# A product-key expert layer's scatter: one-hot rows for four tokens in one instruction, and one buffer for the transposed query

## The chip, the core and the metric

One core of a Trainium2 chip. The metric is the device time of one execution in microseconds (us), as the median of several runs. The core's engines are TensorE (PE in the rows, its weight loads PEld), VectorE (DVE), ScalarE (ACT), GpSimd (POOL) and SyncE (SP), which here only issues transfers. Each engine works through its own queue in order and waits on semaphores of the others.

## The reference

One decoder layer on 1024 prompt tokens and 32 sample tokens, model width 1024, in float32. A mixer (dilated softmax attention, gated linear attention, retention) with its output projection comes first; then a product-key expert layer (PEER) and a final norm. What bears on the change is the expert layer:

```python
qk = (xb @ w_pq).reshape(128, 8, 2, 128)           # 8 heads, two half queries
sc = einsum('thpc,pkc->thpk', qk, keys)            # 128 keys per half
s1, i1 = top_k(sc[:, :, 0], 16); s2, i2 = top_k(sc[:, :, 1], 16)
cand = s1[..., :, None] + s2[..., None, :]
top_s, pos = top_k(cand, 16)                       # 16 of 256 per head
eidx = i1 * 128 + i2                               # at pos: one of 16384 experts
gate = softmax(top_s)
pre = einsum('td,ted->te', xb, u_tab[eidx])
out = einsum('te,ted->td', gelu(pre) * gate, v_tab[eidx])
```

So each token uses 8 x 16 = 128 experts, each an index pair (i1, i2) with a gate.

## The kernel before, in words

The tokens lie in nine tiles: 0 to 7 with 128 prompt tokens each, 8 with the 32 sample tokens. They are handled in five groups, [0], [1, 2], [3, 4], [5, 8] and [6, 7]. For each group the input projection (`inproj`), the mixer (`attention`) and then `outproj` are written down, the next group's `inproj` ahead of the present group's `attention`. `outproj` ends with the expert layer's query:

- For each of 8 heads (`m2`), PE multiplies the two half-query weight tiles with the tokens (L661; L301 for the group of one tile) into a PSUM bank of `pj`, of which there are two. `pj` also serves the input and output projections (L343, L383, L631) and the transposes L259. ScalarE copies the result to the tile `qkT` (L662, or L655).
- For each tile of the group, PE multiplies `qkT` with the keys (L667) into `scr`, one bank; ScalarE copies this to `sc` (L670, two buffers); DVE searches the top 16 of each half (`top16`, L684 to L688).
- `select` then makes the 16 pairs and gates of each head, on DVE for the most part.

From here two paths compute the experts. For tiles 0, 1, 6, 7 and 8 (`gather`) GpSimd fetches each chosen row of the two tables by an indirect DMA (L951, L966), and DVE does a multiply-add over 1024 columns with it (L953, L968). For tiles 2 to 5 (`DENSE`, 512 tokens) all 16384 experts are computed as dense matmuls (`dense`), and what is needed is a matrix of gates, experts by tokens. `scatter` makes it. For each token it builds two one-hot matrices over its 128 pairs: `o2`, where column j of row p is 1 if i2 of pair p is j (DVE, L992, two tokens in one instruction), and `o1`, the same for i1 with the gate as its value (ScalarE, two instructions a token, L997 and L998). A matmul of the two (L999) gives the token's 128x128 gates. Four tokens fill the one PSUM bank `sct`; ScalarE copies it to `st` (L1000), and every eight tokens SyncE stores `st` to `gsd` in DRAM (L1001).

`dense` opens when the mixer's memory is given back. It splits weights and activations into a high and a low part (ScalarE L1017, GpSimd or DVE L1018), and runs over 128 groups of 128 experts: three passes of matmuls up (L1044), Gelu (L1045), the product with the gates `Gt` loaded from `gsd` (L1030, L1048), and, four groups at a time, three passes of matmuls down (L1060), added to `oT` on DVE (L1064).

The order within each engine's queue is not that of the text: at build time a list scheduler plans all instructions with estimated durations (line 1160), highest priority first. Attention, scatter (L677) and dense have raised priorities; the gathers (L1107) have the lowest and are put where the plan sees their engines free. The order is fixed from then on. Where a tile's buffers are all in use, the instruction that writes the next one waits for the last reader of the oldest.

Of the kernel before, what the change touches and what calls it, by code (L numbers as in the profile page):

```python
# [9 lines left out]
F32 = mybir.dt.float32  # L10
# [7 lines left out]
OP = mybir.AluOpType  # L18
# [116 lines left out]
def build(tc, I, O):  # L135
    nc = tc.nc
    ctx = ExitStack()
    V, S, G, PE, SP = nc.vector, nc.scalar, nc.gpsimd, nc.tensor, nc.sync
# [6 lines left out]
    wp = mctx.enter_context(tc.tile_pool(name="wp", bufs=1))  # L145
# [9 lines left out]
    def cload(name, shape, src=None, pool=mc):  # L155
        x = pool.tile(shape, F32, name="c_" + name)
        loads.append(lambda: SP.dma_start(x, I[name] if src is None else src))
        return x

    def bcast(ap, n):  # L160
        return bass.AP(tensor=ap.tensor, offset=ap.offset, ap=[[0, 128], [1, n]])
# [11 lines left out]
    iota128 = cload("iota128", [128, 128], pool=con)  # L173
# [18 lines left out]
    def pj():  # L192
        return ps.tile([128, 512], F32, name="pj", bufs=2)
# [7 lines left out]
    def scr_():  # L201
        return ps.tile([128, 512], F32, name="scr", bufs=1) if SCB == 1 else pj()
# [8 lines left out]
    def na(n=1024):  # L211
        return t4(n, "na", 4)
# [23 lines left out]
    def small(shape, dt=F32, name="sm", bufs=4):  # L236
        return sm.tile(shape, dt, name=name, bufs=bufs)
# [7 lines left out]
    def rms(x, n, nm, junk):  # L245
        ss = con.tile([128, 1], F32, name="ss" + nm, bufs=4)
        S.activation(junk[:n], x, AF.Square, scale=1.0 / 32.0, accum_out=ss[:n])  # L247
        return rstd_of(ss, n, nm)

    def rows(t):  # L250
        return (NP, NS) if t == 8 else (t * 128, 128)

    def transpose_to(dst, c0, src, n):
        for half in range(2):
            p = pj()
            for k in range(4):
                kt = half * 4 + k
                sx = src[half][:n, k * 128:(k + 1) * 128] if isinstance(src, tuple) else src[:n, kt * 128:(kt + 1) * 128]
                PE.transpose(p[:, k * 128:k * 128 + n], sx, ident[:n, :n])  # L259
            S.activation(dst[:, half * 4:half * 4 + 4, c0:c0 + n],  # L260
                         p.rearrange("p (k t) -> p k t", t=128)[:, :, :n], AF.Copy)
# [6 lines left out]
    doff, c = {}, 0  # L268
# [4 lines left out]
    def wtile(src):  # L273
        w = wp.tile([128, 1024], F32, name="w", bufs=WB)
        SP.dma_start(w, src)
        return w.rearrange("p (k m) -> p k m", k=8)

    def wn(src):
        r = []
        for q in range(2):  # L280
            w = wp.tile([128, 1024], F32, name="w", bufs=WB)
            SP.dma_start(w, src[:, q * 1024:(q + 1) * 1024])
            w = w.rearrange("p (k m) -> p k m", k=4)
            r += [w[:, k] for k in range(4)]
        return r
# [328 lines left out]
    def outproj(g):  # L614
        tiles, T, off, oa, sil, nt = g.tiles, g.T, g.off, g.oa, g.sil, g.nt
        oT = wp.tile([128, 8, T], F32, name="hT", bufs=2)
        for i, t in enumerate(tiles):
            transpose_to(oT, off[t], (oa[:, i], sil[:, i]), rows(t)[1])
        x1 = [na() for t in tiles]
        for i, t in enumerate(tiles):  # L620
            r0, n = rows(t)
            SP.dma_start(x1[i][:n], I["x"][r0:r0 + n])
        gffn = na()
        SP.dma_start(gffn, bcast(I["g_ffn"], D))
        for c in range(4):
            w = wn(I["w_outc"][c])
            for i, t in enumerate(tiles):
                n = rows(t)[1]
                p = pj()
                for kt in range(8):  # L630
                    PE.matmul(p[:n, :256], oT[:, kt, off[t]:off[t] + n], w[kt], start=kt == 0, stop=kt == 7)  # L631
                d = x1[i][:n, c * 256:(c + 1) * 256]
                V.tensor_tensor(d, d, p[:n, :256], op=OP.add)
        h2T = wp.tile([128, 8, T], F32, name="hT", bufs=2)
        for i, t in enumerate(tiles):
            r0, n = rows(t)
            SP.dma_start(x1d[r0:r0 + n], x1[i][:n])
            h2 = na()
            rs = rms(x1[i][:n], n, "b", h2)
            V.scalar_tensor_tensor(h2[:n], x1[i][:n], rs[:n], gffn[:n], op0=OP.mult, op1=OP.mult)  # L640
            if t not in DENSE:
                SP.dma_start(h2d[r0:r0 + n], h2[:n])
            transpose_to(h2T, off[t], h2, n)
            if t in DENSE:
                c = doff[t]
                SP.dma_start(h2Td[:, :, c:c + n], h2T[:, :, off[t]:off[t] + n])

        tk = {}
        for i, t in enumerate(tiles):
            tk[t] = (t4p["tk"].tile([128, 2, 8, 16], F32, name="tks", bufs=2), t4p["tk"].tile([128, 2, 8, 16], U16, name="tki", bufs=2))  # L650
        for m2 in range(8):
            qkT = wp.tile([128, 2, T], F32, name="qkT", bufs=2)
            if T == 128:
                p = pair_rows("w_pqT", m2 * 2, h2T)
                S.activation(qkT.rearrange("p m t -> p (m t)"), p[:, :256], AF.Copy)  # L655
            else:
                for m in range(2):
                    w = wtile(I["w_pqT"][m2 * 2 + m])
                    p = pj()
                    for kt in range(8):  # L660
                        PE.matmul(p[:, :T], w[:, kt, :], h2T[:, kt], start=kt == 0, stop=kt == 7)  # L661
                    S.activation(qkT[:, m], p[:, :T], AF.Copy)  # L662
            for i, t in enumerate(tiles):
                n = rows(t)[1]
                p = scr_()
                for m in range(2):
                    PE.matmul(p[:n, m * 128:(m + 1) * 128], qkT[:, m, off[t]:off[t] + n],  # L667
                              keysT[:, m * 128:(m + 1) * 128], start=True, stop=True)
                sc = small([128, 256], name="sc", bufs=2)
                S.activation(sc[:n], p[:n, :256], AF.Copy)  # L670
                ts, ti = tk[t]
                for m in range(2):
                    top16(sc[:n, m * 128:(m + 1) * 128], ts[:n, m, m2], ti[:n, m, m2], n, 128)
        for i, t in enumerate(tiles):
            eg = select(t, *tk[t])
            if t in DENSE:
                with tc.high_priority(-SCP):  # L677
                    scatter(t, *eg)
            else:
                peer_q.append((t,) + eg)  # L680
# [294 lines left out]
    def scatter(t, gfl, gate):  # L975
        n = rows(t)[1]
        p = sct_()
        for q in range(2):
            PE.transpose(p[:, q * 128:q * 128 + n], gfl[:n, q], ident[:n, :n])
        PE.transpose(p[:, 256:256 + n], gate[:n].rearrange("p h k -> p (h k)"), ident[:n, :n])  # L980
        tr = small([128, 4, 128], name="tr", bufs=1)
        S.activation(tr[:, :3, :n], p[:, :384].rearrange("p (q t) -> p q t", t=128)[:, :, :n], AF.Copy)
        S.activation(tr[:, 3, :n], p[:, 256:256 + n], AF.Copy, scale=-1.0)
        for b in range(0, n, TB):
            st = t4p["st"].tile([128, 128, TB], F32, name="st", bufs=STB)
            for q in range(0, TB, 4):
                p = sct_()
                c = b + q
                for k in range(4):
                    if k % 2 == 0:  # L990
                        o2 = small([128, 2, 128], name="o2", bufs=2)
                        V.tensor_tensor(o2, iota128[:, None, :].to_broadcast([128, 2, 128]),  # L992
                                                     tr[:, 1, c + k:c + k + 2, None].to_broadcast([128, 2, 128]),
                                                     op=OP.is_equal)
                    i1, gt, ng = (tr[:, x, c + k:c + k + 1] for x in (0, 2, 3))
                    o1 = small([128, 128], name="o1", bufs=O1B)
                    S.activation(o1, iota128, AF.Abs, scale=-1.0, bias=i1)  # L997
                    S.activation(o1, o1, AF.Relu, scale=ng, bias=gt)  # L998
                    PE.matmul(p[:, k * 128:(k + 1) * 128], o2[:, k % 2], o1, start=True, stop=True)  # L999
                S.activation(st[:, :, q:q + 4], p.rearrange("p (k i) -> p i k", k=4), AF.Copy)  # L1000
            SP.dma_start(gsd[(doff[t] + b) // TB], st.rearrange("p i t -> p (i t)"))  # L1001

# [173 lines left out]
```

## Time and profile before

| | us |
|---|---|
| median of 3 runs | 3195.73 |
| lowest and highest run | 3194.0 and 3199.02 |
| the profiled execution | 3185.95 |
| its span, first to last instruction | 3184.2 |
| PE busy | 2877.7 |
| DVE busy | 2385.3 |
| GpSimd busy | 1916.2 |
| ScalarE busy | 1180.7 |

The busy times are those of the profiled execution. They are sums over stages with different limits, so a change in one stage is to be read from that stage's own rows. The mean granted clock of TensorE was 0.928 of its full speed. In the rows, `out<-in` names what an instruction writes and reads, `x256` is a count, and "idle before" is the time in which the engine stood just before such instructions, with what ended it. In the rows of the scatter `o` stands for both one-hot tiles; L992 is that of `o2`.

### The profile page before, as it was taken

How to read it: one execution, taken by the hardware profiler on the slowest of the kernel's cores; microseconds unless marked ns; L12 is line 12 of the kernel's file. 1: busy time of each engine (PE TensorE's matmuls, PEld its weight loads, DVE VectorE, ACT ScalarE, POOL GpSimd, SP SyncE). 2: the span in 40 equal slices, each digit the busy share in tenths (PEclk: the TensorE clock that was granted, in tenths of full speed). 3: DMA queues.
4: the chain of work that ended last, by engine and by line, in shares of the span. 5: the costliest groups of instructions: out<-in, count | busy, mean ns of one | idle time of the engine just before them, and what ended most of it. 6: DMA issues, size and time to landing. Idle time of an engine off the chain costs nothing. (4 is left out here: it accounts for less than half of the span.)

```text
span 3184.2 us, 40633 instructions
## 1 busy us (share of the span) xinstructions
PE 2877.7 (90%) x13370; PEld 2308.2 (72%) x13370; DVE 2385.3 (75%) x5404; ACT 1180.7 (37%) x2478; POOL 1916.2 (60%) x1447
## 2 busy tenths in 40 slices
PE   7886999997999899997675799999999999999997
PEld 5665777775787556776564688888888888788886
DVE  0366877999789967899999866667676666666775
ACT  2121212321575267776584232222222223222222
POOL 0026564545445434465566587778777788777783
PEclk9798799998899999978876899999999999999998
DMA  7369998999899988989888999999999998999994
GB/s 234 121 226 365 359 357 311 346 337 354 322 346 324 355 306 318 326 292 335 281 330 264 265 313 319 320 312 323 318 325 314 321 317 307 312 317 312 318 330 163
DMA packets 425124, 980.49 MB, mean 308 GB/s; under 512 B 163841, under 2 KB 193042, under 8 KB 424914
## 3 DMA queue, kind: packets, MB, share of 16 engines
q0 software_dynamic: 159808, 580.62, 49.9%
q1 hardware_dynamic: 265106, 397.28, 38.7%
q8 instruction: 106, 1.74, 0.2%
q14 instruction: 104, 0.85, 0.1%
HBM read 925.91 MB, written 51.45 MB: 307 GB/s over the span
## 5 line engine op out<-in xcount | busy, mean ns | idle before, releaser
L951 POOL DMA_INDIRECT g<-in_u_tab,ei x512 | 567.8, 1109 | 443.2 <-DVE g L953 197.3
L966 POOL DMA_INDIRECT g<-in_v_tab,ei x512 | 576.9, 1127 | 418.5 <-DVE gacc L968 123.2
L968 DVE SCALAR_TENSOR_TENSOR gacc<-g,pre,gacc 128x1024 f32<-128x1024 f32 x544 | 710.1, 1305 | 66.3 <-DMA g<-in_v_tab,ei 56.4
L953 DVE SCALAR_TENSOR_TENSOR g<-g,gacc 128x1024 f32<-128x1024 f32 x544 | 654.4, 1217 | 114.7 <-DMA g<-in_u_tab,ei 97.2
L1060 PE MATMUL out<-ah,vh 128*128 128x512 f32 x1024 | 384.8, 392 | 37.0 <-ACT ah L1017 19.1
L1060 PE MATMUL out<-al,vh 128*128 128x512 f32 x1024 | 397.2, 390 | 0.5 <-issue 0.2
L1060 PE MATMUL out<-ah,vl 128*128 128x512 f32 x1024 | 394.1, 390 | 0.1
L1018 POOL TENSOR_TENSOR ul<-raw,uh 128x1024 fp32r<-128x1024 f32 x128 | 310.1, 2426 | 35.1 <-ACT uh L1017 30.6
L1018 POOL TENSOR_TENSOR vl<-raw,vh 128x1024 fp32r<-128x1024 f32 x128 | 307.6, 2418 | 9.6 <-ACT vh L1017 7.9
L1064 DVE TENSOR_TENSOR oT<-oT,out 128x512 f32<-128x512 f32 x248 | 167.3, 684 | 146.3 <-PE out L1060 140.4
L1044 PE MATMUL pre<-hh,ul 128*128 128x512 f32 x1024 | 255.8, 392 | 8.0 <-POOL ul L1018 7.9
L1044 PE MATMUL pre<-hh,uh 128*128 128x512 f32 x1024 | 259.0, 393 | 3.0 <-ACT uh L1017 1.8
L999 PE MATMUL sct<-o,o 128*128 128x128 f32 x1024 | 198.0, 329 | 69.4 <-ACT st L1000 23.5
L1044 PE MATMUL pre<-hl,uh 128*128 128x512 f32 x1024 | 258.0, 389 | 0.0
L1017 ACT ACTIVATE uh<-raw 128x1024 fp32r<-128x1024 f32 x128 | 135.4, 1058 | 324.2 <-DMA raw<-in_uT 288.1
L1060 PEld LDWEIGHTS out<-ah,vh 128*128 128x128 f32 x1024 | 192.8, 189 | 79.6 <-ACT ah L1017 20.6
L999 PEld LDWEIGHTS sct<-o,o 128*128 128x128 f32 x1024 | 165.4, 226 | 114.1 <-ACT o L998 40.9
L1045 ACT ACTIVATE pre<-pre 128x512 f32<-128x512 f32 x128 | 74.5, 582 | 439.2 <-PE pre L1044 402.8
L998 ACT ACTIVATE o<-o,tr 128x128 f32<-128x128 f32 x512 | 230.7, 484 | 0.7
L1044 PEld LDWEIGHTS pre<-hh,ul 128*128 128x128 f32 x1024 | 192.1, 188 | 51.6 <-POOL ul L1018 11.8
L1044 PEld LDWEIGHTS pre<-hh,uh 128*128 128x128 f32 x1024 | 193.8, 190 | 46.2 <-ACT uh L1017 3.5
L661 PE MATMUL pj<-hT,w 128*128 128x256 f32 (+1 forms) x1024 | 223.7, 368 | 0.0
(307 smaller groups left out, 4895.2 us busy)
## 6 DMA issues: line engine op xcount, KB each, us to landing
raw<-in_uT SPq DMA_DIRECT2D x128, 512.0 KB
raw<-in_v_tab SPq DMA_DIRECT2D x128, 512.0 KB
w<-in_w_pqT SPq DMA_DIRECT2D x80, 512.0 KB
gsd<-st SPq DMA_DIRECT2D x64, 512.0 KB
Gt<-gsd SPq DMA_DIRECT2D x16, 2048.0 KB
w<-in_w_inT SPq DMA_DIRECT2D x60, 512.0 KB
w<-in_w_nat SPq DMA_DIRECT2D x60, 512.0 KB
w<-in_w_outc SPq DMA_DIRECT2D x40, 512.0 KB
```

The costliest lines, as they stand in the source:

```text
L661: PE.matmul(p[:, :T], w[:, kt, :], h2T[:, kt], start=kt == 0, stop=kt == 7)
L951: G.indirect_dma_start(out=g, out_offset=None, in_=I["u_tab"], in_offset=bass.IndirectOffsetOnAxis(ap=idx[:, e:e + 1], axis=0))
L953: V.scalar_tensor_tensor(g, g, 1.0, h2, op0=OP.mult, op1=OP.mult, accum_out=pre[:, e:e + 1])
L966: G.indirect_dma_start(out=g, out_offset=None, in_=I["v_tab"], in_offset=bass.IndirectOffsetOnAxis(ap=idx[:, e:e + 1], axis=0))
L968: V.scalar_tensor_tensor(acc, g, act[:, e:e + 1], acc, op0=OP.mult, op1=OP.add)
L998: S.activation(o1, o1, AF.Relu, scale=ng, bias=gt)
L999: PE.matmul(p[:, k * 128:(k + 1) * 128], o2[:, k % 2], o1, start=True, stop=True)
L1017: S.activation(hi, x, AF.Copy)
L1018: eng.tensor_tensor(lo, x, f(hi), op=OP.subtract)
L1044: PE.matmul(p, w[:, kt], x[:, kt], start=kt + n == 0, stop=kt == 7 and n == 2)
L1060: PE.matmul(p, w[:, ds], x, start=j + n == 0, stop=j == EG - 1 and n == 2)
L1064: V.tensor_tensor(oT[:, dt], oT[:, dt], p, op=OP.add)
```

## The change

`o2` is made for four tokens by one DVE instruction of 128x512, in place of two of 128x256; it still has two buffers, now of four tokens each, 2 KB a partition in place of 1 KB. `qkT` has one buffer in place of two; for a group of 256 tokens a buffer is 2 KB a partition. Values are not changed.

```diff
         for m2 in range(8):
-            qkT = wp.tile([128, 2, T], F32, name="qkT", bufs=2)
+            qkT = wp.tile([128, 2, T], F32, name="qkT", bufs=1)
...
                 for k in range(4):
-                    if k % 2 == 0:
-                        o2 = small([128, 2, 128], name="o2", bufs=2)
-                        V.tensor_tensor(o2, iota128[:, None, :].to_broadcast([128, 2, 128]),
-                                                     tr[:, 1, c + k:c + k + 2, None].to_broadcast([128, 2, 128]),
-                                                     op=OP.is_equal)
+                    if k == 0:
+                        o2 = small([128, 4, 128], name="o2", bufs=2)
+                        V.tensor_tensor(o2, iota128[:, None, :].to_broadcast([128, 4, 128]),
+                                        tr[:, 1, c:c + 4, None].to_broadcast([128, 4, 128]), op=OP.is_equal)
...
-                    PE.matmul(p[:, k * 128:(k + 1) * 128], o2[:, k % 2], o1, start=True, stop=True)
+                    PE.matmul(p[:, k * 128:(k + 1) * 128], o2[:, k], o1, start=True, stop=True)
```

## Rows read from the trace of the kernel before

**Rows 1.** The page: busy time of each engine, share of the span, instructions.

```profile
PE 2877.7 (90%) x13370; PEld 2308.2 (72%) x13370; DVE 2385.3 (75%) x5404; ACT 1180.7 (37%) x2478; POOL 1916.2 (60%) x1447
```

**Rows 2.** Busy time by stretch: length, PE, PEld, DVE, ACT, POOL, clock, DMA, GB/s.

```profile
900.00:1100.00 200.00, 187.89 (x954) 144.83 (x954) 195.06 (x680) 95.22 (x256) 101.89 (x85) 0.97 0.94 335
1100.00:1400.00 300.00, 283.66 (x1564) 206.43 (x1565) 238.96 (x665) 213.01 (x556) 137.78 (x102) 0.94 0.89 317
1400.00:1560.00 160.00, 111.65 (x505) 91.15 (x504) 154.05 (x409) 104.99 (x262) 99.55 (x70) 0.74 0.87 311
1560.00:1640.00 80.00, 67.49 (x368) 60.08 (x368) 75.00 (x262) 56.15 (x154) 37.04 (x39) 0.95 0.88 311
1640.00:1705.00 65.00, 36.02 (x131) 29.57 (x131) 63.41 (x184) 53.92 (x133) 45.48 (x31) 0.53 0.81 280
1705.00:1850.00 145.00, 107.76 (x446) 86.00 (x445) 126.60 (x271) 40.84 (x47) 87.64 (x66) 0.87 0.88 268
1850.00:3160.00 1310.00, 1298.66 (x5699) 1068.28 (x5698) 895.60 (x1198) 370.22 (x477) 1022.43 (x726) 1.00 0.93 312
```

**Rows 3.** The same by stretch, of the one-hot line L992 alone.

```profile
900.00:1100.00 200.00, 15.91 (x40) 0.97 0.94 335
1100.00:1400.00 300.00, 36.73 (x90) 0.94 0.89 317
1400.00:1560.00 160.00, 18.26 (x46) 0.74 0.87 311
1560.00:1640.00 80.00, 11.07 (x29) 0.95 0.88 311
1640.00:1705.00 65.00, 11.58 (x28) 0.53 0.81 280
```

**Rows 4.** Timeline around the scatter's end: SyncE's Gt load, PE's next matmul.

```profile
1709.38 0.37 SPq L1030 DMA_DIRECT2D Gt<-gsd  x1
...
1738.79 1.65 PE L1060 MATMUL out<-ah,vh 128*128 128x512 f32 x3 [18.64 <-ACT ah L1017]
```

**Rows 5.** Instruction groups: count, busy us, mean ns, idle before and its causes.

```profile
L968 DVE SCALAR_TENSOR_TENSOR gacc<-g,pre,gacc 128x1024 f32<-128x1024 f32 x544 | 710.1, 1305 | 66.3 <-DMA g<-in_v_tab,ei 56.4 <-issue 5.5 <-DMA g<-in_v_tab,eip 0.5
...
L992 DVE TENSOR_TENSOR o<-c_iota,tr 128x256 f32<-128x256 f32 x256 | 103.4, 415 | 45.5 <-PE sct L999 38.7 <-ACT tr L982 4.7 <-issue 1.0
...
L1018 DVE TENSOR_TENSOR hl<-raw,hh 128x512 fp32r<-128x512 f32 x8 | 5.4, 688 | 2.3 <-ACT hh L1017 2.3
```

**Rows 6.** Timeline of DVE, two narrow and two wide instructions: start, us.

```profile
825.07 0.76 DVE L992 TENSOR_TENSOR o<-c_iota,tr 128x256 f32<-128x256 f32 x2 [4.70 <-ACT tr L982]
...
1742.07 1.29 DVE L1018 TENSOR_TENSOR al<-pre,ah 128x512 fp32r<-128x512 f32 x2
```

**Rows 7.** Waits from 1560 to 1640, then 1640 to 1705: us, times, longest.

```profile
PE sct L999 <- DVE o L992: 7.1, 3, 3.0
...
PE sct L999 <- DVE o L992: 15.0, 7, 4.6
```

**Rows 8.** Timeline of PE and ACT, third group; then pj's share of a stretch.

```profile
982.89 0.61 PE L667 MATMUL scr<-c_keysT,qkT 128*128 128x128 f32 x4
...
984.48 0.64 ACT L662 ACTIVATE qkT<-pj 128x256 f32<-128x256 f32 x2
...
1011.78 0.61 PE L667 MATMUL scr<-c_keysT,qkT 128*128 128x128 f32 x4
...
984.90:1011.80 26.90, 14.76 (x64) 11.22 (x64) 0.00 (x0) 3.22 (x7) 0.94 0.83 283
```

**Rows 9.** Timeline from 1668 to 1690: GpSimd's splits, DVE's instructions beside them.

```profile
1668.55 8.25 POOL L1018 TENSOR_TENSOR vl<-raw,vh 128x1024 fp32r<-128x1024 f32 x3 [6.45 <-ACT vh L1017]
...
1668.57 0.41 DVE L992 TENSOR_TENSOR o<-c_iota,tr 128x256 f32<-128x256 f32 x1
...
1682.68 3.89 DVE L968 SCALAR_TENSOR_TENSOR gacc<-g,pre,gacc 128x1024 f32<-128x1024 f32 x1
...
1683.12 2.36 POOL L1018 TENSOR_TENSOR vl<-raw,vh 128x1024 fp32r<-128x1024 f32 x1
```

## The prediction

> **What bounds the kernel now.** Start with the busy line of the page: TensorE (PE) is busy 90% of the span, VectorE (DVE) 75% [rows 1]. That mean mixes two regimes, so the stretches come next [rows 2]. From 1850 us on PE works 1298.7 of 1310 us: there nothing that the change touches can help, and only the moment at which this stage begins counts. Ahead of it, DVE is the fuller engine: 195.1 of 200 us from 900 to 1100, 154.1 of 160, 75.0 of 80 and 63.4 of 65 from 1400 to 1705, and 126.6 of 145 up to 1850. Between 1100 and 1400 it is the other way round: PE 283.7 of 300, DVE 239.0.
>
> The change sits in the scatter, which runs from 825 to 1705. The third view, the one-hot line alone by stretch [rows 3], says how many of its 256 instructions lie where DVE is full: 40 + 46 + 29 + 28 = 143. The 90 between 1100 and 1400 lie where PE is the limit.
>
> What follows the scatter matters too. The load of the gate slab Gt is issued at 1709.38, behind the last scatter store, and PE, after three expert groups that need no gate, stands 18.64 us until 1738.79 [rows 4]. So the end of the scatter, or the DVE queue up to the first gate product, sets the start of the PE-bound stage.
>
> **The change, part by part.**
>
> *One-hot rows.* 256 instructions of 128x256 become 128 of 128x512. A narrow one takes 415 ns, and the nearest row for a wide one is the split of h2, also 128x512 float32 with both inputs in SBUF: 688 ns [rows 5]. Taken alone, a pair saves 2 x 415 - 688 = 142 ns. But instructions overlap in the queue: two narrow ones end after 0.76 us, so the second adds 0.345, and two wide ones (another 128x512 row) after 1.29 us, so the second adds 0.602 [rows 6]. By what the queue sees, a pair saves 2 x 0.345 - 0.602 = 0.088 us. I take the second price, since DVE is full and its neighbours overlap. Where DVE is full there are 143 / 2 = 71.5 pairs: 6.3 us, with 10.2 as the other end. The 45 pairs between 1100 and 1400 I cost at nothing: PE hides them; without that cover they would give 4.0 us more.
>
> *Deeper lookahead.* Two buffers now hold eight tokens instead of four, so DVE can make the rows of a group while the two before it are still used. In 1560 to 1705 PE waited 7.1 + 15.0 = 22.1 us for one-hot rows [rows 7]: that is the upper end. Zero is the lower. DVE itself is idle in the two stretches only 5.0 + 1.6 = 6.6 us [rows 2], and a full engine cannot be hurried by a buffer: I take 6.6. Behind it, ScalarE would be late next: it is busy 53.9 of 65 us in the last stretch [rows 2].
> The first matmul of a group now waits for all four rows, 0.688 instead of 0.415 us after the instruction starts; since the rows are made a group ahead, this lies beside the other group's work, and with that cover gone it would be 0.27 us on each group of the last two stretches, (29 + 28) / 2 = 28.5 groups, 7.8 us.
>
> *One buffer for the transposed query.* No instruction is added; a wait is. ScalarE's copy L662 of the next head may write only when all score matmuls L667 of the head before have read. Queued behind it on ScalarE are the scatter's own activations, and PE waits for it through the projection banks pj, of which there are two; the weight loads on the SyncE queue wait for PE in turn. The worst place in the trace is the third group of tiles [rows 8]: both copies of the last head run at 984.48, just after a head's scores end at 982.89 + 0.61, so even two buffers were full. With one buffer they must wait for the scores of the head between, 1011.78 + 0.61: 27.9 us later. (Four score groups run after 984.48, two for each of the two heads left; the one at 1011.78 is the second.) PE work on pj inside that hold is 14.8 us [rows 8], all of which would be pushed out. PE is idle 200 - 187.9 = 12.1 us in the stretch [rows 2] and can take up that much. I cost the wait at 14.8 - 12.1 = 2.7 us. Its ends are 0 (the order is written anew and other PE work fills in) and 27.9 us (PE stands still for the whole hold).
>
> *The rest.* No transfer is added or removed, and SyncE and GpSimd issue the same DMAs. The o2 buffers grow by as much as the query tile gives back for groups of 256 tokens, so the tiles of the last stage meet the same neighbours. The order of every queue is planned at build time from estimated durations, so it is planned anew; no row prices this, and I bound it by the length of one gather step either way, about 1.3 us [rows 5], per place where it matters, which is inside the bounds above.
>
> **The sum.** -6.3 - 6.6 + 2.7 = -10.2 us. The profiled execution took 3185.95 us (span 3184.2), so it would take 3175.8. The median of the runs is 3195.73, 9.8 above that execution; on it the sum gives **3185.5 us**. A change under 0.2% (6.4 us) cannot be told from none here.
>
> **A rule that speaks against it.** While GpSimd splits weights (8.25 us for three from 1668.55, and 2.36 from 1683.12), a DVE multiply-add with two SBUF inputs took 3.89 us at 1682.68 against its mean of 1.305; yet a one-hot instruction started at 1668.57 took its usual 0.41 [rows 5, 9]. The Trainium skill (SBUF — State Buffer, section "SBUF: two separate sides") says that a two-input DVE instruction and a GpSimd instruction that reads SBUF exclude each other for a whole instruction, whichever starts first. By that rule the multiply-add was held, as the row has it, and a longer one-hot instruction would meet a split more often; the one-hot row at 1668.57 does not bear it out. By the rule the sum would be -4.2 us (worked out below from rows), by the one-hot row it stays -10.2.
>
> **The rivals.**
>
> *Slower: the query buffer decides.* For it: the copies at 984.48 ran as soon as the second buffer came free, the scores trail DVE's top-16 search, and PE is the limit right after, from 1100 [rows 2, 8]. Against it: the order is planned with the single buffer known, so PE may be given other work. If PE stands through one hold of 27.9 us, and 6.3 + 6.6 = 12.9 come back, the result is +15.0: 3210.7 us. It decides as soon as the holds cost more than 12.9 us.
>
> *No change: the gathers fill the gap.* The multiply-adds of the gathers (L953, L968) have the lowest priority and go where the plan sees DVE free; one takes 1.3 us [rows 5]. Ten freed microseconds are eight such steps pulled ahead of the last stage, which is PE-bound and gains nothing from losing them [rows 2]. For it: DVE is full in the last stretches although the gathers have no deadline there. Against it: a step pulled ahead also needs its transfer earlier. Time: 3195.7.
>
> *No change: GpSimd holds the wide rows.* The splits cover 8.25 + 2.36 = 10.6 of the last 65 us [rows 9], so of 28 / 2 = 14 wide instructions 2.3 are met, each held by up to 3.89 - 1.305 = 2.6 us: 6.0 us back, net -4.2, 3191.5 us. The Trainium skill's exclusion rule above is this mechanism.
>
> *Faster by more: the scatter was the chain.* If the first gate product waits for Gt and not for DVE's queue, all 22.1 us of PE's waits come off, with the dearer price of the rows: -22.1 - 10.2 = -32.3, 3163.4 us. For it: PE's stand of 18.64 us right after the load [rows 4]. Against it: DVE has hardly a gap there [rows 2].
>
> **How the numbers follow.** The forecast has 0.40, in its bounds 3182 to 3192, of which 0.31 lies more than 0.2% below; the large gain has 0.10; no change through gathers 0.12; through GpSimd 0.04; slower 0.34, of which 0.01 within. So faster 0.41, same 0.26, slower 0.33. With chance on both sides the range goes from the large gain to the slower rival, widened by what the shown runs spread about their median (1.7 below, 3.3 above): 3161.7 to 3214. Beyond either end I leave about 0.1.
>
> **What would show it.** Right: the one-hot line with 128 instructions near 690 ns; PE's waits for it in the last stretches well under 22 us; the last scatter store some 10 us earlier, and the PE-bound stage as long as before (1310 us from its 1850 mark). Wrong: PE or ScalarE waiting at L662, L661 or L259 while scores L667 are outstanding, and scatter beginning later than 825; or more multiply-adds of the gathers ahead of 1705 with the scatter's end unmoved; or one-hot instructions of over 1 us.

## The result, and the profile after

The changed kernel takes 3217.82 us (median of 8 runs, 3205.66 to 3227.35) against 3196.61 (8 runs, 3184.58 to 3201.0) for the kernel before on the same chip. The ratio is 1.0071, 95% interval 1.0057 to 1.0084: slower by 22.7 us, 18.2 to 26.8. Below, each ratio is turned into microseconds with 3195 us. The execution that was profiled after lies near its median, the one of before 11 us under its own, so the two traces stand 35.2 us apart where the medians stand 21.2: a lateness that is read from them is some 14 us too large at the end.

The page of the changed kernel, its span and busy line, against [rows 1]:

```profile
span 3219.4 us, 40372 instructions
PE 2897.2 (90%) x13370; PEld 2322.8 (72%) x13370; DVE 2377.8 (74%) x5276; ACT 1177.9 (37%) x2478; POOL 1921.9 (60%) x1447
```

TensorE has the same 13370 instructions, DVE has 128 fewer and 7.5 us less work, and the span is 35.2 us longer all the same. Of these, 19.5 stand in TensorE's own busy time (2897.2 us against 2877.7): the same instructions took longer, at a mean granted clock of 0.923 instead of 0.928. The other 15.7 are time in which TensorE stood. The busy time by stretch says where it fell behind. First the two stretches ahead of those of [rows 2], for the kernel before (length, PE, PEld, DVE, ACT, POOL, clock, DMA share, GB/s):

```profile
640.00:825.00 185.00, 158.50 (x795) 120.97 (x793) 170.98 (x494) 44.64 (x94) 89.34 (x78) 0.87 0.91 334
825.00:900.00 75.00, 71.54 (x387) 60.51 (x386) 58.78 (x156) 52.88 (x144) 36.92 (x33) 0.89 0.98 372
```

The same view of the changed kernel, with the stretches of [rows 2]:

```profile
640.00:825.00 185.00, 149.00 (x751) 112.14 (x750) 169.53 (x490) 43.47 (x92) 93.70 (x78) 0.87 0.91 326
825.00:900.00 75.00, 72.69 (x365) 59.75 (x364) 52.80 (x121) 48.16 (x125) 32.79 (x30) 0.86 0.94 336
900.00:1100.00 200.00, 183.76 (x936) 142.61 (x935) 187.09 (x654) 100.24 (x274) 102.54 (x84) 0.95 0.92 324
1100.00:1400.00 300.00, 286.39 (x1524) 206.58 (x1522) 238.03 (x588) 207.96 (x541) 142.82 (x104) 0.95 0.90 325
1400.00:1560.00 160.00, 118.11 (x541) 93.69 (x539) 152.11 (x385) 92.85 (x226) 99.97 (x66) 0.75 0.90 324
1560.00:1640.00 80.00, 65.02 (x328) 57.57 (x329) 69.81 (x251) 51.53 (x137) 33.56 (x37) 0.86 0.74 260
1640.00:1705.00 65.00, 41.86 (x201) 35.98 (x199) 64.25 (x214) 56.27 (x145) 39.71 (x28) 0.69 0.79 267
1705.00:1850.00 145.00, 95.25 (x384) 76.52 (x385) 133.04 (x275) 50.95 (x92) 89.04 (x69) 0.79 0.89 275
1850.00:3160.00 1310.00, 1293.77 (x5667) 1065.67 (x5666) 896.04 (x1198) 375.73 (x483) 1029.55 (x730) 1.00 0.94 315
```

Up to 640 the two run level. From 640 to 825, before any scatter, the changed kernel does 9.5 us less PE work and 44 matmuls fewer, while DVE does nearly as much as before: PE has begun to wait. By itself this is no measure of the loss, since the kernel e8 below does even less there (147.0 us) and takes no longer than before. Taken over all stretches up to 1850 it is 44 + 22 + 18 + 40 - 36 + 40 - 70 + 62 = 120 matmuls behind; at the last stretch's 5699 in 1310 us [rows 2] that is 27.6 us. A matmul is not a unit of time, but the timeline at the scatter's end of the changed kernel says the same:

```profile
1731.45 0.32 SPq L1000 DMA_DIRECT2D gsd<-st  x1
...
1737.92 0.37 SPq L1029 DMA_DIRECT2D Gt<-gsd  x1
...
1770.11 1.65 PE L1059 MATMUL out<-ah,vh 128*128 128x512 f32 x3 [21.89 <-ACT ah L1016]
```

The Gt load goes out at 1737.92 instead of 1709.38, and the first matmul behind a gate product runs at 1770.11 instead of 1738.79 [rows 4]. In these two traces, 28 to 31 of the 35.2 us are there when the PE-bound stage begins; that stage itself adds little.

The one-hot rows did what they were to do. Instruction groups of the changed kernel, against [rows 5]:

```profile
L992 DVE TENSOR_TENSOR o<-c_iota,tr 128x512 f32<-128x512 f32 x128 | 90.6, 710 | 41.2 <-PE sct L998 40.8
L1017 DVE TENSOR_TENSOR hl<-raw,hh 128x512 fp32r<-128x512 f32 x8 | 5.3, 685 | 0.9 <-ACT hh L1016 0.9
```

128 instructions of 710 ns in place of 256 of 415: 90.6 us instead of 103.4. PE's waits in the scatter of the last tiles, from 1560 to its end, here 1735 (name, us, times, longest), against [rows 7]:

```profile
PE sct L998 <- ACT st L999: 15.7, 12, 2.1
PE sct L998 <- ACT o L997: 11.7, 6, 4.6
PE sct L998 <- DVE o L992: 10.6, 4, 3.4
```

The wait for rows fell from 22.1 to 10.6 us. The same view of before has 8.4 us behind the slab copy and 11.1 behind ScalarE's half of the rows; these are now 15.7 and 11.7. Of 11.5 us saved 7.9 came back as waits for ScalarE.

What is new stands around the query copies. Waits from 571 to 1705, kernel before:

```profile
ACT qkT L662 <- PE pj L661: 55.4, 31, 4.0
ACT sc L670 <- DVE tmp L685: 23.0, 15, 6.0
```

and the changed kernel:

```profile
ACT sc L670 <- DVE tmp L685: 39.7, 17, 8.0
ACT qkT L662 <- PE pj L661: 22.3, 15, 4.0
...
PE scr L667 <- ACT qkT L662: 13.4, 5, 8.7
ACT qkT L662 <- PE scr L667: 6.2, 3, 3.8
```

The copies L662 used to wait for nothing but their own projection. Now they also wait for the scores of the head before (6.2 us), ScalarE waits 16.7 us longer at the score copy L670, and PE waits 13.4 us for the query. One place shows how these three hang together. Timeline of the changed kernel, engine by engine as they start:

```profile
1619.04 0.61 PE L667 MATMUL scr<-c_keysT,qkT 128*128 128x128 f32 x4
...
1623.10 1.21 DVE L953 SCALAR_TENSOR_TENSOR g<-g,gacc 128x1024 f32<-128x1024 f32 x1
...
1625.46 1.23 DVE L953 SCALAR_TENSOR_TENSOR g<-g,gacc 128x1024 f32<-128x1024 f32 x1 [0.54 <-DMA g<-in_u_tab,eip]
...
1627.48 0.27 DVE L685 MATCH_REPLACE8 tmp<-tks,sc 128x128 f32<-128x128 f32 x1
...
1627.84 0.38 ACT L670 ACTIVATE sc<-scr 128x256 f32<-128x256 f32 x1 [7.29 <-DVE tmp L685]
...
1628.12 0.66 ACT L662 ACTIVATE qkT<-pj 128x256 f32<-128x256 f32 x2
...
1628.55 0.80 PE L667 MATMUL scr<-c_keysT,qkT 128*128 128x128 f32 x2 [8.68 <-ACT qkT L662]
```

The last scores of a head end at 1619.65, and the single query tile is free. The copies of the next head run 8.5 us later, because in ScalarE's queue they stand behind the score copy L670, which waits 7.29 us for a score tile that DVE's top-16 still reads (with gather steps L953 in between). PE waits 8.68 us for them. The Trainium skill (PSUM — Partial Sum Buffer, section "Engine vs sequencer instructions") says that the queues of ScalarE, VectorE and GpSimd are strictly first in, first out; this trace agrees, with two copies that ran 0.28 us behind the start of the instruction that had stood 7.29 us.

With two tiles the copies may stand ahead of both score copies of a head. With one they cannot stand ahead of the first: they overwrite what the second scores read, and the one score bank is free for these only behind the first score copy. Ahead of the second score copy they can stand, and 23 us later in the same timeline they do:

```profile
1649.83 0.61 PE L667 MATMUL scr<-c_keysT,qkT 128*128 128x128 f32 x4
...
1651.24 0.62 ACT L662 ACTIVATE qkT<-pj 128x256 f32<-128x256 f32 x2
...
1653.83 0.38 ACT L670 ACTIVATE sc<-scr 128x256 f32<-128x256 f32 x1 [0.80 <-DVE tmp L685]
```

So the wait of 7.29 us at 1627.84 is the order that was planned with one tile, and not the tile alone.

### The profile page after: what moved, and what is told of

It reads as the page before. It is cut to its first block, busy times and chain, and to the rows that moved or that the text cites. A ratio compares the mean times of both kernels' runs of the same rounds, so it can differ in the third digit from the quotient of the medians.

```text
span 3219.4 us, 40372 instructions
## 1 busy us (share of the span) xinstructions
PE 2897.2 (90%) x13370; PEld 2322.8 (72%) x13370; DVE 2377.8 (74%) x5276; ACT 1177.9 (37%) x2478; POOL 1921.9 (60%) x1447
## 5 line engine op out<-in xcount | busy, mean ns | idle before, releaser
L968 DVE SCALAR_TENSOR_TENSOR gacc<-g,pre,gacc 128x1024 f32<-128x1024 f32 x544 | 697.3, 1282 | 76.9 <-DMA g<-in_v_tab,ei 70.3
L953 DVE SCALAR_TENSOR_TENSOR g<-g,gacc 128x1024 f32<-128x1024 f32 x544 | 653.8, 1215 | 117.2 <-DMA g<-in_u_tab,ei 107.5
```

Of the source, the lines that this page charges most:

```text
L953: V.scalar_tensor_tensor(g, g, 1.0, h2, op0=OP.mult, op1=OP.mult, accum_out=pre[:, e:e + 1])
L968: V.scalar_tensor_tensor(acc, g, act[:, e:e + 1], acc, op0=OP.mult, op1=OP.add)
```

## The experiments

Each is an edit of the kernel before, unless said otherwise; ratios are against the kernel before on the same chip. "Single tile" is the one query buffer.

**The two edits apart, and the rows with two buffers.** Two wide row buffers beside two whole query tiles take 2 KB per partition more than the kernel before. So the wide rows were tried with one buffer, in the memory of before, and with two where one of six gather buffers (GB) made room.

```
e1:  qkT = wp.tile([128, 2, T], F32, name="qkT", bufs=1)
e2:  o2 = small([128, 4, 128], name="o2", bufs=1), made once for four tokens
e3:  GB = 5
e4:  GB = 5, and o2 [128, 4, 128] with bufs=2; qkT keeps bufs=2
```

> Only the query tile loses its second buffer; the one-hot rows stay at two tokens. Query theory (the single buffer holds the projection banks and the main chain falls behind): about +20 us against the kernel before, 3210 to 3225, with the third group's output projection some 15 us late as in the changed kernel. Scatter theory (the wide rows let the scatter overtake the main chain): within 6 us of before, 3190 to 3203. Plan theory (no single part, the whole plan comes out otherwise): anything, and the two parts do not add up to the change.

> Only the one-hot rows are made wide, in one buffer of four tokens, the same memory and the same lookahead of four tokens as before; the query tile keeps two buffers. Query theory: no loss of the change's size; 3190 to 3205, a few us lost to waiting for the whole buffer. Scatter theory: without the deeper lookahead the scatter cannot overtake, so no loss either, 3190 to 3205; DVE waits for PE at the one-hot line go up. Plan theory: anything within 30 us either way.

> A control: the kernel before with five gather buffers in place of six, which gives back 4 KB a partition for the next run. All theories: the gathers are not what bounds, so 3190 to 3210; what it differs from before is the offset for the next run.

> The control with the one-hot rows wide in two buffers and the query tile left with two: the first part of the change alone. Query theory: within 6 us of the control, or faster by the 5 to 10 us that the prediction gave the wide rows. Scatter theory: about 20 us slower than the control, with the scatter of the third group on time and the output projections late. Plan theory: anything.

e1: 3221.54 us, ratio 1.0075 (1.0049 to 1.0101), +24 us: the single tile alone carries the whole loss. e2: 3192.3, ratio 0.9983 (0.9965 to 1.0001), -5.4: a gain, if any. e3: 3294.64, ratio 1.03 (1.0271 to 1.0328), +96, where no change was expected. e4: 3269.67, ratio 1.0239 (1.021 to 1.0269), 20 us less than e3, uncertain by 13. So the query tile hurts and the rows do not: the scatter theory, by which the rows are at fault, fell. Whether the parts add is not settled. With e2 for the rows they make 24 - 5 = +19, with e4 against e3 they make 24 - 20 = +4, uncertain by 15, and the change is at +22.7. So the plan theory did not fall. Nor is the 20 a price of the rows in the kernel before, since e3 and e4 end on late gathers (last section). What this pair does show is the Gt load, in e3 and then in e4:

```profile
1704.24 0.37 SPq L1030 DMA_DIRECT2D Gt<-gsd  x1
...
1675.85 0.38 SPq L1029 DMA_DIRECT2D Gt<-gsd  x1
```

Beside two query tiles the wide rows in two buffers end the scatter 28 us sooner. Beside one tile they do not move it: 1737.22 in e1, 1737.92 in the change. These are single traces; the kernel before and the control e10, which take equally long, stand 13 us apart in the same place (1709.38 and 1722.15).

**What the single tile waits for.** Four score tiles instead of two behind it (memory as before), the same with wide rows in one buffer, the changed kernel with the query in two half tiles, and a mixture.

```
e5:  qkT bufs=1;  sc = small([128, 256], name="sc", bufs=4)
e6:  e5, and o2 [128, 4, 128] with bufs=1
e7:  the changed kernel with qkT = [wp.tile([128, T], F32, name="qkT", bufs=2) for m in range(2)]
e8:  such halves with bufs=3, sc bufs=3, o2 [128, 4, 128] with bufs=1
```

> Before with one query buffer (as in the first experiment, +24 us) and four score tiles sc instead of two; memory as before. Release theory: the single query buffer comes free only with the last scores L667 of a head, those wait for the one score bank scr, that for the copy L670, and that for an sc tile that DVE's top-16 still reads; with four sc tiles the copies no longer wait, so the loss goes: 3191 to 3203 us, ACT's wait at L670 for DVE tmp L685 falls from 25 us (before) and 40 us (after) to under 12, and the third group's select is within 8 us of before's. Handoff theory: one buffer costs a fixed round trip per head (scores end, copy, next scores) whatever stands behind it: 3214 to 3228 us, PE's wait at L667 for qkT L662 stays over 10 us.

> The same with the one-hot rows four tokens wide in one buffer (second experiment, -5 us); memory as before. Release theory: 3186 to 3200 us, the two parts add. Handoff theory: 3209 to 3224 us.

> The changed kernel with the query kept as two half tiles of 1 KB in two buffers in all, so that a half is handed back by its own scores; memory as in the changed kernel. Release theory: both halves of a head are handed back by the scores of the same last token tile, a tenth of a microsecond apart, so nothing changes: 3211 to 3224 us. Granularity theory (the first half's copy is held by the second half's scores): 3195 to 3206 us.

> Before with wide rows in one buffer, three half query tiles (3 KB instead of 4) and three sc tiles (3 KB instead of 2). Release theory: the first half of the next head finds a free buffer and the second needs one more top-16 of slack, which the third sc tile gives: 3186 to 3201 us. Handoff theory: half of the loss stays: 3200 to 3212 us.

e5: 3199.8 us, ratio 1.0013 (0.9993 to 1.0032), +4: some 20 of the 24 us gone. Waits of e5 from 571 to 1705:

```profile
ACT sc L670 <- DVE tmp L685: 13.6, 7, 3.0
...
PE scr L667 <- ACT qkT L662: 3.3, 4, 1.5
```

Both are what the release theory asked for in direction: less waiting at the score copy (26.1 us in e1, 13.6 here), less at PE (6.4 in e1, 3.3 here). The first row stands a little over the "under 12" that was expected, and it is not the price of the tile: in e1, with the whole loss, it is hardly above the 23.0 of before. Nor did the third group come back to where it was, as expected: its last scores end at 987 us, 59 ahead of before. The plan is another one, not that of before with a wait less. e6: 3188.08, ratio 0.9971 (0.9955 to 0.9988), -9.3 us, faster than both kernels. e8: 3198.04, ratio 1.0009 (0.9993 to 1.0025): no difference. e7 went against the release theory: 3199.63, ratio 1.0019 (0.9997 to 1.0041), where 3211 or more was expected. Handing the query back by halves in the same memory takes 17 us off the changed kernel.

**Halves, a control, and the other end of the chain.**

```
e9:  qkT as half tiles, bufs=2 (two rows wide as before)
e10: qkT as half tiles, bufs=4
e11: sc bufs=1; qkT bufs=2
e12: qkT as half tiles, bufs=2; sc bufs=4; o2 [128, 4, 128] with bufs=1
```

> Before (rows two wide) with the query as two half tiles of 1 KB, two in all: the changed kernel's query memory, handed back by halves. Granularity theory: the loss of the whole single tile (+24 us) was that of handing it back as one; by halves it is +4 to +14 us (3198 to 3210), and the first dense matmul comes within 12 us of before's. Wide-rows theory of the run before (the changed kernel with halves, +6 us): the recovery there came from the rows, and halves with narrow rows stay at +18 to +30 us (3212 to 3224).

> Control: before with the query as half tiles, four in all: as much memory and as much lookahead as before, each half handed back by itself, and 32 activations of some 0.4 us where the one-tile groups had one per pair. Resource theory (what counts is how far the copies can run ahead of the scores): 3190 to 3202 us, no measurable change. Reordering theory (any edit here shifts the order of instructions that is fixed at build time, and that alone moves the time by ten or twenty us): further than 8 us from before on either side.

> Before with one score tile sc instead of two, the query's two buffers kept. Release theory (the path from query to top-16 has a slack of buffers, and the query's and the scores' are the same slack): losing one head-and-tile of it costs as losing one query buffer did, +12 to +40 us (3206 to 3234), ACT's wait at L670 for DVE tmp L685 rises from 25 us to over 45. Query-only theory (what costs is the pj banks held by the waiting copies of the query, not the slack behind): under +8 us (3189 to 3202).

> Query as two half tiles (2 KB), four sc tiles, wide rows in one buffer; memory as before. Release and granularity theories together: at least as fast as one whole query tile with the same (-9 us): 3178 to 3190 us, ratio 0.995 to 0.998. If the gain there was an accident of order: 3192 to 3204 us.

e9: 3210.44 us, ratio 1.0046 (1.003 to 1.0062), +14.7: the halves alone take 9 of the 24 us off, and the wide rows in two buffers take off 8.6 more (e7). Each of these two steps is about as large as its uncertainty; together, 17.9 us, they are clear of it. The first dense matmul runs 14 us later than before, where within 12 was expected. e10: 3196.06, ratio 1.0005 (0.999 to 1.0021): the control stands still, so the halves by themselves do not move the time (they add 8 activations, those of the one-tile group, not 32). e11: 3201.66, ratio 1.0017 (0.9999 to 1.0036), +5: a score tile less is not what a query tile less is. Its wait at L670 for DVE did not rise over 45 us but fell to 15.8, presumably because the order planned for one score tile puts the copies later, where they need not wait. That half of the release theory fell. e12: 3198.66, ratio 1.0008 (0.9992 to 1.0024), where 3178 to 3190 was expected: the good parts do not add up, and part or all of e6's gain may be its particular order.

**The banks.** Both halves of a head's query in one pj bank, with one activation, for two query tiles and for one; then with the version of e6.

```
     p = pj()
     for m in range(2):
         ... PE.matmul(p[:, m * T:(m + 1) * T], w[:, kt, :], h2T[:, kt], ...)
     S.activation(qkT.rearrange("p m t -> p (m t)"), p[:, :2 * T], AF.Copy)
e13: qkT bufs=2      e14: qkT bufs=1      e15: qkT bufs=1, sc bufs=4, o2 wide with bufs=1
```

> Control for the next: before with both halves of a head's query in one pj bank (512 columns) and one activation of 512 columns for the two of 256; two query tiles. Both theories: within 10 us of before (3183 to 3203): 24 activations fewer, but the first half is copied only when the second is done.

> The same with one query tile. Bank theory: the waiting copy holds one bank of two, the other goes on serving the other tile groups, and the single tile costs at most 10 us more than the run before. Chain theory: the banks do not matter, and the single tile costs 15 to 30 us more than the run before, as it did with two banks.

> One bank, one query tile, four score tiles, wide rows in one buffer; memory as before. Bank theory: as fast as the two-bank form of it or faster, 3178 to 3189 us (ratio 0.9945 to 0.998). Chain theory: nothing gained by the bank, 3184 to 3196.

e13: 3229.69 us, ratio 1.0122 (1.01 to 1.0145), +39, where both theories had it within 10 of before (the activations saved are 32, not 24). e14: 3214.56, ratio 1.0054 (1.0033 to 1.0074), +17: here the single tile is 22 us faster than two tiles. e15: 3195.51, ratio 0.9997 (0.9984 to 1.001), in the range of the chain theory and without the gain of e6. The pair of e13 and e14 does not decide between the theories: its control moved more than the thing to be measured. What it does show is that the price of the single tile is no constant. It belongs to one arrangement of the copies.

**The score copies off ScalarE's queue.** DVE makes the 72 copies of the scores, with two query tiles and with one.

```
-                S.activation(sc[:n], p[:n, :256], AF.Copy)
+                V.tensor_copy(sc[:n], p[:n, :256])
e16: qkT bufs=2      e17: qkT bufs=1
```

> Control for the next: before with the 72 copies of the scores (L670) made by DVE instead of ScalarE, two query tiles. DVE is the fuller engine ahead of 1705, so it is slower by part of 72 x 0.38 = 27 us: 3200 to 3228 us in both theories.

> The same with one query tile. Queue theory (the next head's copies stand on ScalarE behind a score copy that waits for DVE's top-16, and PE's next scores behind them): with the score copies on DVE the single tile costs at most 8 us more than the run before. Other-cause theory (the order planned with one tile is worse whatever queue the score copy is on): 15 to 30 us more than the run before.

e16: 3211.16 us, ratio 1.0049 (1.0032 to 1.0067), in its range. e17: 3243.29, ratio 1.0139 (1.0109 to 1.0169). The single tile costs 0.009 x 3195 = 29 us here, as much as in e1: the queue theory fell, and the place behind L670 is not the price. But with the score copies gone from ScalarE, its wait is in plain sight. Waits from 571 to 1705, e16:

```profile
ACT qkT L662 <- PE pj L661: 60.4, 32, 5.4
...
ACT qkT L662 <- PE scr L667: 3.6, 5, 2.0
```

and e17:

```profile
ACT qkT L662 <- PE scr L667: 45.6, 8, 15.2
ACT qkT L662 <- PE pj L661: 21.7, 10, 4.1
```

ScalarE stands 45.6 us, up to 15.2 at a time, for the scores of the head before to be read, against 3.6 with two tiles. In the changed kernel the same lateness seems to hide in the row of L670, behind which the copies stand.

## Why the prediction was wrong

**The step that failed** is the +2.7 us for the one query buffer. It measured +24 (e1), nine times as much. That this is close to the upper end of 27.9 which stood beside it is luck, since PE did not stand through a hold. Three things in it were off.
- *The place.* It was priced at one hold, in the third group around 984 [rows 8]. That hold came. In the changed kernel the copies of the group's last head run at 1029.18 instead of 984.48, straight behind the scores of the head between:

```profile
1028.44 0.71 PE L667 MATMUL scr<-c_keysT,qkT 128*128 128x128 f32 x4
...
1029.18 0.66 ACT L662 ACTIVATE qkT<-pj 128x256 f32<-128x256 f32 x2 [2.18 <-PE scr L667]
```

  Yet PE worked 38.7 of the 44.7 us from 984.5 to 1029.2, and from 900 to 1100 it did 187.9 - 183.8 = 4.1 us less work than before (11.0 less in e1): more than the 2.7, and not the whole loss. It is also 9.5 us behind from 640 to 825, ahead of the stretches in which the step looked, and another 12.5 from 1705 to 1850, where the scatter now ends.
- *The cover.* 12.1 us of PE idleness in a stretch was set against the held work. But DVE is full in the same stretch [rows 2], and scores, score copy and top-16 wait for one another. Idle time of PE that is caused by DVE is no room for work that waits for DVE. This is argued; no run prices it.
- *One hold for all.* The three groups of 256 tokens and the one of 160 have 32 heads, and any but the first of a group can hold. e17 shows 8 waits that add up to 45.6 us.

**The rival that happened** is the slower one, in its sign and in the wait that it names: the copies wait for the scores of the head before for 6.2 us in the change, 5.3 in e1, 45.6 in e17. Its one hold of 27.9 us, with PE standing through it, is not what happened. Its size, +15.0, was short of the +22.7 measured, in part because the 12.9 us that it took back did not come: with the query tile whole, the wide rows gave 1.3 us (the change against e1), uncertain by 9.

**The one-hot rows, -6.3.** 710 ns against the 688 taken from [rows 5]: the nearest row was right. The group's busy time fell by 12.8 us over 128 pairs, 0.10 us a pair, near the 0.088 that was chosen.

**The deeper lookahead, -6.6.** PE's wait for rows fell by 11.5 us, but ScalarE took 7.9 back, as the step had it ("ScalarE would be late next"). The rows' worth as a whole came out as -1.3 in the change, -5.4 with one buffer (e2), -8.6 beside half queries (e7 against e9) and -20 with five gather buffers, where late gathers end the kernel. Each is uncertain by 6 to 13 us, so they do not show that the worth differs from place to place; the sum's -12.9 was too much where it was used.

**No change through the gathers; faster by more.** Neither: in the change the scatter's end moved the other way. The second has something for it all the same: beside two query tiles (e4 against e3) the Gt load does come 28 us sooner.

**GpSimd holds the wide rows.** Small, and near its size: 2.3 held of 14 and 6.0 us were forecast. Two of the 128 wide instructions were held, 2.36 and 2.84 us; in the timeline of the changed kernel each stands beside a split on GpSimd:

```profile
1569.01 2.53 POOL L1017 TENSOR_TENSOR ul<-raw,uh 128x1024 fp32r<-128x1024 f32 x1 [0.60 <-ACT uh L1016]
1569.72 2.36 DVE L992 TENSOR_TENSOR o<-c_iota,tr 128x512 f32<-128x512 f32 x1
...
1682.61 7.02 POOL L1017 TENSOR_TENSOR vl<-raw,vh 128x1024 fp32r<-128x1024 f32 x3 [0.40 <-ACT vh L1016]
1687.34 2.84 DVE L992 TENSOR_TENSOR o<-c_iota,tr 128x512 f32<-128x512 f32 x1
...
1699.91 3.37 POOL L1017 TENSOR_TENSOR vl<-raw,vh 128x1024 fp32r<-128x1024 f32 x1
1700.39 0.68 DVE L992 TENSOR_TENSOR o<-c_iota,tr 128x512 f32<-128x512 f32 x1
```

That is 2.36 + 2.84 - 2 x 0.69 = 3.8 us in all. The Trainium skill's rule (SBUF — State Buffer, section "SBUF: two separate sides") that such a pair exclude each other for a whole instruction agrees with the first two; at 1700.39 the one-hot instruction ran at its usual length while the split took 3.37 us instead of 2.53, which agrees with the rule only if DVE came first, and spans on GpSimd are too rough to say so. For the same reason the prediction's row was read too plainly: by the recorded starts its multiply-add of 3.89 us began 0.44 us ahead of the split at 1683.12 [rows 9].

**The signs that were named.** The one-hot line (128 instructions, 710 ns) and PE's wait for it (10.6 us) came out as for a right forecast. The last scatter store, forecast some 10 us earlier, went out 27.5 us later (1731.45, against 1703.91 in the timeline of before), and the waits of the query copies came as for a wrong one.

**The range** ended at 3214, 4 us short of the result: it took the slower rival at +15.0 with the full gain of the rows taken off, and not at its own upper end.

**What stays open.** That the single tile costs 24 us is shown (e1). That it ties the next head's copies to the scores of the head before is seen in the waits (e17 above all). That more score tiles take the loss away is shown once (e5), in a plan of its own. That DVE paces those scores is argued. How the loss is handed on to PE is not settled, and neither is how much of it is the new order and how much the wait itself: the order of every queue is planned anew for each of these kernels, a wait that the plan foresees may be in no row (e11), and in the one-bank pair the sign turned round. An order held fixed while the tile count changes was not tried: the order of before cannot run with one tile, since its copies stand ahead of the scores that they would wait for.

## What to carry to other kernels

A buffer in a chain that crosses three engines should be priced over all its uses, and not by one hold against the idle time of the engine ahead of it: ask what must finish before it is handed back, who does that, and how full that engine is. When memory must be found for a wider tile, two other ways were better here. The same 2 KB of query handed back as halves were 17 us faster than the change (e7), and one query tile, four score tiles and one wide row buffer, in the memory of before, were faster than both kernels (e6, ratio 0.9971), though two near relatives were not (e12, e15). And where a planner fixes the order, price each part with a control beside it: of those here one stood still (e10), and one moved by 39 us (e13).

## What the runs showed that was not expected

One gather buffer of six is worth 96 us (e3). Over half of it lies at the very end, where a last normalisation waits for gathers that were not done in time. Waits over the whole span of e3:

```profile
DVE g L953 <- DMA g<-in_u_tab,ei: 198.0, 129, 6.6
DVE gacc L968 <- DMA g<-in_v_tab,ei: 138.1, 82, 7.1
...
ACT g L247 <- DVE gacc L968: 57.1, 2, 54.3
```

DVE's waits for gathered rows were 97.2 and 56.4 us before; with five buffers they are 198.0 and 138.1, and ScalarE stands 54.3 us for the last gather sum, against 2.0 before. With six buffers the PE-bound stage covers the gathers, with five it does not.

And two activations of 256 columns made into one of 512 behind both halves (e13) cost 39 us, although it issues 32 instructions fewer. That the half which is ready first was worth copying at once is a guess; with one query tile the same edit cost nothing (e14 against e1).
